# Stick-breaking attention: one set of products with values per pair of heads, q and k split once and copied by DMA, scan in place

## The chip, the cores and the metric

The program runs on one core of a Trainium2 chip: TensorE (PE) multiplies matrices, VectorE (DVE) and ScalarE (ACT) work elementwise, GpSimd (POOL) and SyncE (SP) issue most transfers. The metric is device time in microseconds, the median of three executions.

## The reference

Four sub-layers run on 512 tokens of width 1024: retention, a gated ConvFFN, stick-breaking attention, a second ConvFFN. The change touches the third alone. It has 16 heads of 64 columns; for each block of 128 queries the blocks of keys are swept from the last to the first:

```python
z = jnp.einsum('bhqd,bhkd->bhqk', qb, kb) * scale
log1m = jnp.where(mask, jax.nn.log_sigmoid(-z), 0.0)
excl = lax.cumsum(log1m, axis=3, reverse=True) - log1m
log_a = jax.nn.log_sigmoid(z) + excl + suffix[..., None]
a = jnp.where(mask, jnp.exp(log_a), 0.0)
acc = acc + jnp.einsum('bhqk,bhkd->bhqd', a, vb)
```

Each weight is thus sigmoid(z) of its key times the product of sigmoid(-z) over the keys between it and the query. Everything is float32.

## The kernel before

Activations lie transposed, features on partitions, tokens along the row. A float32 product that is to be exact is made of three products on rounded parts: hi = the operand cast to fp32r, lo = the rest (`split`, `parts`, `mm3`). Weights arrive in 512 KB pieces by SyncE (`chunk`) and are split by ScalarE (L130) and VectorE (L131).

The heads are worked in eight pairs, here called pair 0 to pair 7. A step is one head of a pair with one block of 128 queries, so a pair has eight steps, from the longest row of keys (four blocks, 512) to the shortest (one block, 128). In a step, `sb_weights` makes z with two products (L591), two sigmoids (L593, L594), a scan on VectorE that multiplies sigmoid(-z) up from the right end (L597, into tile cs) and the product of both (L601). One step later `sb_transpose` turns the blocks on TensorE (L609) and copies them out (L610, over the tile of sigmoid(-z)). `sb_av` multiplies them with the values (L617) once both heads of a query block are there: `o` gathers 128 columns of queries at a time, the first head on partitions 0 to 63, the second on 64 to 127. After the last block `o` is split into hi and lo (L108, L109).

q and k of a pair (`sb_qk`) are 128 rows, 64 for each head. A product for z has 128 partitions: q's hi above its lo, against k's hi twice and then k's lo twice. So for every head hi is cast (L558, and L562 for the second copy of k) and lo is subtracted (L560, L563) on 64 partitions at a time: six casts and six subtractions per pair.

Between the steps, `sb_fill` gives TensorE other work: in pairs 0 to 5 q and k for the pair two ahead, in pairs 0, 2 and 4 values as well, in pairs 6 and 7 the output projection. `FILL` is how many pieces go into each step. The program's instructions are recorded and then ordered by a scheduler, so the order on each engine is not that of the code; each engine works its own list strictly in order. Buffers come from pools that hand out a fixed number per tag: a tile waits until the last reader of its buffer is done. GpSimd's queue issues, early in the program, copies and sums of FFN weights (tile sum); in the attention it only sets one column of cs to zero per step (L596).

Of the kernel before, what the change touches and what calls it, by code (L numbers as in the profile page):

```python
# [9 lines left out]
F32 = mybir.dt.float32  # L10
# [5 lines left out]
P = 128  # L16
# [20 lines left out]
class Kernel:  # L37
# [12 lines left out]
    def __init__(self, ctx, tc, t):  # L50
        self.tc, self.nc, self.t = tc, tc.nc, t
        self.const = ctx.enter_context(tc.tile_pool(name="const", bufs=1))
        self.wp = ctx.enter_context(tc.tile_pool(name="wp", bufs=1))
        self.ap = ctx.enter_context(tc.tile_pool(name="ap", bufs=1))
        self.dp = ctx.enter_context(tc.tile_pool(name="dp", bufs=1, space=bass.MemoryType.DRAM))
        self.ps = ctx.enter_context(tc.tile_pool(name="ps", bufs=1, space=bass.MemoryType.PSUM))
        self.n = 0
        self.pp = None
        self.att_pool()
        self.phase("mix")  # L60

    def att_pool(self):
        self.pa = self.tc.tile_pool(name=self.name("pa"), bufs=1, space=bass.MemoryType.PSUM, reuse_waits="tile")
# [17 lines left out]
        return f"{s}_{self.n}"  # L81

    BUFS = {"xh": 8, "xl": 8, "tt": 8, "rr": 2}
    PHASE = {"qk": 8, "vv": 8, "yy": 16, "pp": 8, "cs": 4, "ar": 2, "oh": 5, "ol": 5}

    def sb(self, tag, cols=S, dt=F32):
        pool, bufs = (self.ap, self.BUFS) if tag in self.BUFS else (self.ph, self.PHASE)
# [432 lines left out]
    def ffn(self, l, last):  # L520
# [11 lines left out]
                s += 1  # L532
        self.swap_pool()
        self.down(l, a, s, last)
        self.phase("mix" if last is not None else None)
        return a


    def sb_qk(self, p, out, first=None):
# [3 lines left out]
        for i in range(2):  # L543
# [8 lines left out]
                    yield  # L552
            x = self.sb("tt")
            nc.vector.tensor_mul(x, ps, self.r)
            for e in range(2):
                own, other = slice(e * DH, e * DH + DH), slice(DH - e * DH, 2 * DH - e * DH)
                hi = self.sb("qk", S, F32R)
                nc.scalar.copy(hi[own], x[own])  # L558
                lo = hi if i == 0 else self.sb("tt", S, F32R)
                nc.vector.tensor_sub(lo[other], x[own], hi[own].bitcast(F32))  # L560
                if i == 1:
                    nc.scalar.copy(hi[other], x[own])  # L562
                    nc.vector.tensor_sub(lo[own], x[own], hi[own].bitcast(F32))  # L563
                heads[e] += [hi] if i == 0 else [hi, lo]
        out.append(heads)

    def sb_v(self, c, out):
# [15 lines left out]
    def sb_weights(self, qk, i, e):  # L583

        nc = self.nc
        n = (i + 1) * P
        nz = max(n, 256)
        q, kh, kl = qk[e]
        z = self.psum("z", 2)
        for m, k in enumerate((kh, kl)):  # L590
            nc.tensor.matmul(z[:, :nz], q[:, i * P : (i + 1) * P], k[:, :nz], start=m == 0, stop=m == 1)  # L591
        sg, bt = self.sb("pp"), self.sb("pp")
        nc.scalar.activation(sg[:, :n], z[:, :n], AF.Sigmoid, scale=-0.125)  # L593
        nc.scalar.activation(bt[:, :n], z[:, :n], AF.Sigmoid, scale=0.125)  # L594
        left = self.sb("cs", S + P)
        nc.gpsimd.memset(left[:, n : n + 1], 0.0)  # L596
        nc.vector.tensor_tensor_scan(  # L597
            left[:, :n][:, ::-1], sg[:, :n][:, ::-1], self.diag[:, S - n :][:, ::-1],
            0.0, op0=ALU.mult, op1=ALU.max,
        )  # L600
        nc.vector.tensor_mul(bt[:, :n], bt[:, :n], left[:, 1 : n + 1])  # L601
        return sg, bt

    def sb_transpose(self, i, sg, bt):
        nc = self.nc
        n = (i + 1) * P
        tp = self.psum("tp", 2)
        for j in range(i + 1):
            nc.tensor.transpose(tp[:, j * P : (j + 1) * P], bt[:, j * P : (j + 1) * P], self.ident)  # L609
        nc.vector.tensor_copy(sg[:, :n], tp[:, :n])  # L610
        return sg

    def sb_av(self, o, p, i, v, aT):
        for j in range(i + 1):
            for e in range(2):
                h = (2 * p + e) % 8
                self.nc.tensor.matmul(  # L617
                    o[e * DH : (e + 1) * DH, i * P : (i + 1) * P], v[p // 4 * NT + j][:, h * DH : (h + 1) * DH],
                    aT[e][:, j * P : (j + 1) * P], start=j == 0, stop=j == i,
                )  # L620

    def stick_breaking(self):


        first = self.first4("sfirst")
        qk, v, os = [], [], []
        self.rc = self.token_major_r()
        for p in range(2):
            for _ in self.sb_qk(p, qk, first[2 * p : 2 * p + 2]):
                pass  # L630
# [1 line left out]
            pass  # L632
        self.swap_pool()
        steps = [(p, i, e) for p in range(NPAIR) for i in reversed(range(NT)) for e in range(2)]
        wt, aT, fill, o = {}, {}, iter(()), None
        for t in range(len(steps) + 2):
            if t < len(steps):
                p, i, e = steps[t]
# [4 lines left out]
                wt[t] = self.sb_weights(qk[p], i, e)  # L643
            for _ in range(rate):
                next(fill, None)
            if 1 <= t <= len(steps):
                aT[t - 1] = self.sb_transpose(steps[t - 1][1], *wt.pop(t - 1))
            if t >= 2 and steps[t - 2][2] == 1:
                p, i, _ = steps[t - 2]
                if i == NT - 1:  # L650
                    o = self.one()
                self.sb_av(o, p, i, v, (aT.pop(t - 3), aT.pop(t - 2)))
                if i == 0:
                    os.append(self.split(o, ("yy", "yy")))
        for _ in fill:
            pass
        self.swap_pool()
# [189 lines left out]
```

## Time and profile before

| | |
|---|---|
| runs | 1377.50, 1377.51, 1378.72 us; median 1377.51 |
| profiled execution | 1378.58 us, span 1376.8 us |
| PE, share of the span busy | 99% (7208 matmuls) |
| DVE | 74%, 1014.2 us |
| ACT | 45%, 618.8 us |
| POOL | 4%, 51.4 us |
| TensorE clock granted | 0.999 of 2.4 GHz |

The shares are means over stages with different limits. A matmul's busy time includes its way through the array, so the next one starts well before it ends; what TensorE really needs is read from the starts. Times of instructions are from one profiled execution, 1.1 us above the median.

### The profile page before, as it was taken

What the parts mean: (1) busy time and instruction counts of PE and PEld (TensorE: products, weight loads), DVE (VectorE), ACT (ScalarE), POOL (GpSimd) and SP (SyncE); (2) the same over time, 40 slices, a digit from 0 to 9 for tenths busy, and PEclk for the clock granted to TensorE, in tenths of its full rate; (3) what the DMA queues carried; (4) which work ended last, traced back from release to release, by engine and by line L of the source; (5) the groups of instructions that cost most, each with busy time, mean ns of one, the idle gap of its engine ahead of it and who ended that gap; (6) DMA issues with size and microseconds to landing.
All of it is one profiled execution on the core that took longest, in us unless ns stands there. A gap on an engine that the chain in (4) does not pass through costs nothing.

```text
span 1376.8 us, 18478 instructions
## 1 busy us (share of the span) xinstructions
PE 1364.9 (99%) x7208; PEld 1157.4 (84%) x7208; DVE 1014.2 (74%) x1416; ACT 618.8 (45%) x876; POOL 51.4 (4%) x134
## 2 busy tenths in 40 slices
PE   9999999999999999999999999999999999999997
PEld 7888888888888889889988888787788899889887
DVE  7774564664769877678667779889789886787765
ACT  6443333433346444344344655554356443444434
POOL 1222210000000000000000000000000000000000
PEclk9999999999999999999999999999999999999999
DMA  8999983131233335324522421120133335235121
GB/s 301 312 281 273 276 220 96 49 115 62 64 94 119 107 108 179 112 92 124 164 72 69 138 92 51 58 62 24 39 123 122 101 117 181 74 105 182 54 69 62
DMA packets 53190, 170.22 MB, mean 124 GB/s; under 512 B 6000, under 2 KB 8176, under 8 KB 53104
## 3 DMA queue, kind: packets, MB, share of 16 engines
q1 hardware_dynamic: 42880, 136.25, 30.9%
q0 software_dynamic: 8704, 31.46, 9.3%
q10 hardware_dynamic: 1520, 1.33, 0.3%
q8 instruction: 57, 0.93, 0.3%
q14 instruction: 29, 0.24, 0.1%
HBM read 166.92 MB, written 33.55 MB: 146 GB/s over the span
## 4 chain that ended last, share of the span: by engine, by line
PE 96%; DVE 3%; issue 0%; ACT 0%; DVEq 0%
PE acc L139 23%; PE acc L137 23%; PE acc L138 23%; PE x L455 6%; PE att L137 4%; PE att L138 4%; PE att L139 4%; PE z L455 3%; PE acc L455 2%; PE one L617 2%; PE z L591 1%; PE tp L609 1%; DVE cs L597 1%; DVE lo L131 0%; DVE tt L563 0%; DVE tt L560 0%
## 5 line engine op out<-in xcount | busy, mean ns | idle before, releaser
L130 ACT CAST hi<-raw 128x1024 fp32r<-128x1024 f32 (+2 forms) x277 | 268.3, 969 | 432.4 <-PE acc L138 274.5
L138 PE MATMUL acc<-xl,hi 128*128 128x512 f32 x960 | 374.5, 390 | 0.0
L139 PE MATMUL acc<-xh,lo 128*128 128x512 f32 x960 | 374.4, 390 | 0.0
L137 PE MATMUL acc<-xh,hi 128*128 128x512 f32 x960 | 374.2, 390 | 0.0
L131 DVE TENSOR_TENSOR lo<-raw,hi 128x1024 fp32r<-128x1024 f32 (+2 forms) x277 | 309.4, 1118 | 55.4 <-ACT hi L130 53.7
L139 PEld LDWEIGHTS acc<-xh,lo 128*128 128x128 f32 x960 | 180.2, 188 | 37.5 <-issue 0.5
L137 PEld LDWEIGHTS acc<-xh,hi 128*128 128x128 f32 x960 | 180.3, 188 | 36.8 <-issue 0.5
L138 PEld LDWEIGHTS acc<-xl,hi 128*128 128x128 f32 x960 | 180.3, 188 | 36.0
L407 DVE SCALAR_TENSOR_TENSOR tt<-tt,vec,tt 128x511 f32<-128x511 f32 (+1 forms) x176 | 131.3, 747 | 4.0 <-ACT tt L405 1.4
L404 DVE TENSOR_TENSOR tt<-acc,rr 128x512 f32<-128x512 f32 x80 | 55.1, 688 | 75.6 <-PE acc L139 75.6
L189 DVE TENSOR_TENSOR x<-x,acc 128x512 f32<-128x512 f32 x72 | 48.9, 685 | 53.5 <-PE acc L139 53.5
L139 PE MATMUL acc<-hi,xl 128*128 128x512 f32 (+1 forms) x256 | 86.0, 336 | 0.0
L138 PE MATMUL acc<-lo,xh 128*128 128x512 f32 (+1 forms) x256 | 85.9, 336 | 0.0
L137 PE MATMUL acc<-hi,xh 128*128 128x512 f32 (+1 forms) x256 | 85.9, 336 | 0.0
L405 ACT ACTIVATE tt<-tt,vec 128x512 f32<-128x512 f32 x88 | 71.5, 812 | 11.0 <-DVE tt L404 10.0
L139 PE MATMUL acc<-yy,lo 128*128 128x512 f32 x192 | 75.2, 392 | 0.0
L137 PE MATMUL acc<-yy,hi 128*128 128x512 f32 x192 | 75.1, 391 | 0.0
L138 PE MATMUL acc<-yy,hi 128*128 128x512 f32 x192 | 75.0, 391 | 0.0
L455 PE MATMUL x<-oh,hi 128*128 128x256 f32 x240 | 68.2, 284 | 0.0
L455 PE MATMUL x<-ol,hi 128*128 128x256 f32 x240 | 67.9, 283 | 0.0
L455 PE MATMUL x<-oh,lo 128*128 128x256 f32 x240 | 67.9, 283 | 0.0
L597 DVE TENSOR_TENSOR_SCAN cs<-pp,diag 128x512 f32<-128x512 f32 (+3 forms) x64 | 52.1, 819 | 3.3 <-ACT pp L593 2.2
(173 smaller groups left out, 2254.7 us busy)
## 6 DMA issues: line engine op xcount, KB each, us to landing
raw<-in_up SPq DMA_DIRECT2D x80, 512.0 KB, 3.9
sum<-in_fast POOLq DMA_DIRECT2D x36, 512.0 KB, 8.7
raw<-sum SPq DMA_DIRECT2D x24, 512.0 KB, 3.4
raw<-in_fast SPq DMA_DIRECT2D x18, 512.0 KB, 3.6
raw<-in_rv SPq DMA_DIRECT2D x16, 512.0 KB, 6.0
raw<-in_rg SPq DMA_DIRECT2D x16, 512.0 KB, 4.3
raw<-in_rout SPq DMA_DIRECT2D x16, 512.0 KB, 4.2
raw<-in_rqk SPq DMA_DIRECT2D x12, 512.0 KB, 6.3
```

Source lines behind the costliest of these rows:

```text
L130: nc.scalar.copy(hi, raw)
L131: nc.vector.tensor_sub(lo, raw, hi.bitcast(F32))
L137: mm(out, a[0], b[0], start=start, stop=False)
L138: mm(out, a[0], b[1], start=False, stop=False)
L139: mm(out, a[1], b[0], start=False, stop=stop)
L189: self.nc.vector.tensor_add(self.x[m], self.x[m], ps)
L404: nc.vector.tensor_mul(u, ps, self.r)
L405: nc.scalar.activation(c, u, AF.Identity, scale=w[2], bias=w[3])
L407: nc.vector.scalar_tensor_tensor(c[:, i:], u[:, : S - i], w[2 - i], c[:, i:], op0=ALU.mult, op1=ALU.add)
L455: mm(out[:, :Q], a[ai], b[bi], start=start and k + i == 0, stop=k == nk - 1 and i == 2, skip_group_check=not start)
L597: nc.vector.tensor_tensor_scan(left[:, :n][:, ::-1], sg[:, :n][:, ::-1], self.diag[:, S - n :][:, ::-1], 0.0, op0=ALU.mult, op1=ALU.max,)
L617: self.nc.tensor.matmul(o[e * DH : (e + 1) * DH, i * P : (i + 1) * P], v[p // 4 * NT + j][:, h * DH : (h + 1) * DH], aT[e][:, j * P : (j + ...
```

## The change

The cast of q or k to hi and the subtraction for lo are made once for both heads, on 128 partitions, into one tile hl (hi in the first 512 columns, lo behind it; one buffer). GpSimd's queue then copies the 64 rows of a head to where z wants them: for q four copies of 64 x 512 (hi to the upper, lo to the lower half, for each head), for k four of 64 x 1024 (hi and lo together, to both halves, for each head).

The scan writes over its own input, a tile sg that is kept for each of the eight steps and has one column of zeros behind it, set once. bt has two buffers.

The transposed weights of a head go into one tile `at` for all four query blocks, laid out so that what stands against one block of keys is contiguous: 512 queries for the first block, 384, 256 and 128 for the others. `sb_av` runs once per pair, behind the second step of the next pair, with eight products. The tiles of this phase have a pool of their own, and the results of the later four pairs take buffers xh and xl.

```diff
@@ -81,7 +81,7 @@
         return f"{s}_{self.n}"
 
     BUFS = {"xh": 8, "xl": 8, "tt": 8, "rr": 2}
-    PHASE = {"qk": 8, "vv": 8, "yy": 16, "pp": 8, "cs": 4, "ar": 2, "oh": 5, "ol": 5}
+    PHASE = {"qk": 8, "vv": 8, "yy": 16, "pp": 8, "cs": 4, "ar": 2, "oh": 5, "ol": 5, "sq": 2, "sk": 4, "hl": 1, "bt": 2, "at": 2, "oo": 8}
 
     def sb(self, tag, cols=S, dt=F32):
         pool, bufs = (self.ap, self.BUFS) if tag in self.BUFS else (self.ph, self.PHASE)
@@ -532,7 +532,7 @@
                 s += 1
         self.swap_pool()
         self.down(l, a, s, last)
-        self.phase("mix" if last is not None else None)
+        self.phase("sb" if last is not None else None)
         return a
 
 
@@ -552,16 +552,23 @@
                     yield
             x = self.sb("tt")
             nc.vector.tensor_mul(x, ps, self.r)
-            for e in range(2):
-                own, other = slice(e * DH, e * DH + DH), slice(DH - e * DH, 2 * DH - e * DH)
-                hi = self.sb("qk", S, F32R)
-                nc.scalar.copy(hi[own], x[own])
-                lo = hi if i == 0 else self.sb("tt", S, F32R)
-                nc.vector.tensor_sub(lo[other], x[own], hi[own].bitcast(F32))
-                if i == 1:
-                    nc.scalar.copy(hi[other], x[own])
-                    nc.vector.tensor_sub(lo[own], x[own], hi[own].bitcast(F32))
-                heads[e] += [hi] if i == 0 else [hi, lo]
+            hl = self.sb("hl", 2 * S, F32R)
+            nc.scalar.copy(hl[:, :S], x)
+            nc.vector.tensor_sub(hl[:, S:], x, hl[:, :S].bitcast(F32))
+            move = lambda to, of: nc.gpsimd.dma_start(to, of)
+            if i == 0:
+                q = self.sb("sq", 2 * S, F32R)
+                for e in range(2):
+                    own = slice(e * DH, e * DH + DH)
+                    for a in range(2):
+                        move(q[a * DH : a * DH + DH, e * S : e * S + S], hl[own, a * S : a * S + S])
+                    heads[e].append(q[:, e * S : e * S + S])
+            else:
+                for e in range(2):
+                    k = self.sb("sk", 2 * S, F32R)
+                    for a in range(2):
+                        move(k[a * DH : a * DH + DH], hl[e * DH : e * DH + DH])
+                    heads[e] += [k[:, :S], k[:, S:]]
         out.append(heads)
 
     def sb_v(self, c, out):
@@ -589,42 +596,49 @@
         z = self.psum("z", 2)
         for m, k in enumerate((kh, kl)):
             nc.tensor.matmul(z[:, :nz], q[:, i * P : (i + 1) * P], k[:, :nz], start=m == 0, stop=m == 1)
-        sg, bt = self.sb("pp"), self.sb("pp")
+        sg, bt = self.sg[i][e], self.sb("bt")
         nc.scalar.activation(sg[:, :n], z[:, :n], AF.Sigmoid, scale=-0.125)
         nc.scalar.activation(bt[:, :n], z[:, :n], AF.Sigmoid, scale=0.125)
-        left = self.sb("cs", S + P)
-        nc.gpsimd.memset(left[:, n : n + 1], 0.0)
+
         nc.vector.tensor_tensor_scan(
-            left[:, :n][:, ::-1], sg[:, :n][:, ::-1], self.diag[:, S - n :][:, ::-1],
+            sg[:, :n][:, ::-1], sg[:, :n][:, ::-1], self.diag[:, S - n :][:, ::-1],
             0.0, op0=ALU.mult, op1=ALU.max,
         )
-        nc.vector.tensor_mul(bt[:, :n], bt[:, :n], left[:, 1 : n + 1])
-        return sg, bt
-
-    def sb_transpose(self, i, sg, bt):
+        nc.vector.tensor_mul(bt[:, :n], bt[:, :n], sg[:, 1 : n + 1])
+        return bt
+
+
+    ROW = S - P
+
+    def sb_transpose(self, i, bt, aT):
         nc = self.nc
         n = (i + 1) * P
         tp = self.psum("tp", 2)
         for j in range(i + 1):
             nc.tensor.transpose(tp[:, j * P : (j + 1) * P], bt[:, j * P : (j + 1) * P], self.ident)
-        nc.vector.tensor_copy(sg[:, :n], tp[:, :n])
-        return sg
-
-    def sb_av(self, o, p, i, v, aT):
-        for j in range(i + 1):
+        to = aT[:, i * P : i * P + (i + 1) * self.ROW].rearrange("p (j q) -> p j q", q=self.ROW)[:, :, :P]
+        nc.vector.tensor_copy(to, tp[:, :n].rearrange("p (j q) -> p j q", q=P))
+
+    def sb_av(self, o, p, v, aT):
+        for j in range(NT):
             for e in range(2):
                 h = (2 * p + e) % 8
                 self.nc.tensor.matmul(
-                    o[e * DH : (e + 1) * DH, i * P : (i + 1) * P], v[p // 4 * NT + j][:, h * DH : (h + 1) * DH],
-                    aT[e][:, j * P : (j + 1) * P], start=j == 0, stop=j == i,
+                    o[e * DH : (e + 1) * DH, j * P :], v[p // 4 * NT + j][:, h * DH : (h + 1) * DH],
+                    aT[e][:, j * (P + self.ROW) : j * self.ROW + S], start=j == 0, stop=j == NT - 1, skip_group_check=True,
                 )
 
     def stick_breaking(self):
 
 
+        nc = self.nc
         first = self.first4("sfirst")
         qk, v, os = [], [], []
         self.rc = self.token_major_r()
+        self.sg = [[self.ph.tile([P, (i + 1) * P + 1], F32, name=f"sg{i}{e}") for e in range(2)] for i in range(NT)]
+        for i in range(NT):
+            for e in range(2):
+                nc.gpsimd.memset(self.sg[i][e][:, (i + 1) * P :], 0.0)
         for p in range(2):
             for _ in self.sb_qk(p, qk, first[2 * p : 2 * p + 2]):
                 pass
@@ -632,7 +646,7 @@
             pass
         self.swap_pool()
         steps = [(p, i, e) for p in range(NPAIR) for i in reversed(range(NT)) for e in range(2)]
-        wt, aT, fill, o = {}, {}, iter(()), None
+        wt, fill = {}, iter(())
         for t in range(len(steps) + 2):
             if t < len(steps):
                 p, i, e = steps[t]
@@ -643,15 +657,14 @@
                 wt[t] = self.sb_weights(qk[p], i, e)
             for _ in range(rate):
                 next(fill, None)
+            if t % 8 == 1 and t > 8:
+                o = self.one()
+                self.sb_av(o, t // 8 - 1, v, aT)
+                os.append(self.split(o, ("oo", "oo") if len(os) < 4 else ("xh", "xl")))
             if 1 <= t <= len(steps):
-                aT[t - 1] = self.sb_transpose(steps[t - 1][1], *wt.pop(t - 1))
-            if t >= 2 and steps[t - 2][2] == 1:
-                p, i, _ = steps[t - 2]
-                if i == NT - 1:
-                    o = self.one()
-                self.sb_av(o, p, i, v, (aT.pop(t - 3), aT.pop(t - 2)))
-                if i == 0:
-                    os.append(self.split(o, ("yy", "yy")))
+                if t % 8 == 1:
+                    aT = [self.sb("at", (NT + 1) * self.ROW) for _ in range(2)]
+                self.sb_transpose(steps[t - 1][1], wt.pop(t - 1), aT[steps[t - 1][2]])
         for _ in fill:
             pass
         self.swap_pool()
```

On TensorE, the end of pair 0's longest query blocks before: a transpose (tp), the first eight products with values (one), and the next z.

```order
L609 MATMUL tp_6722<-diag,pp_6646 128x128 x3
L617 MATMUL one_6727<-pp_6554,vv_6439 64x128
L617 MATMUL one_6727<-pp_6602,vv_6439 64x128
L617 MATMUL one_6727<-pp_6554,vv_6466 64x128
L617 MATMUL one_6727<-pp_6602,vv_6466 64x128
L617 MATMUL one_6727<-pp_6554,vv_6493 64x128
L617 MATMUL one_6727<-pp_6602,vv_6493 64x128
L617 MATMUL one_6727<-pp_6554,vv_6520 64x128
L617 MATMUL one_6727<-pp_6602,vv_6520 64x128
L591 MATMUL z_6736<-qk_6393,qk_6385 128x256
L591 MATMUL z_6736<-tt_6395,qk_6385 128x256
```

The same engine in the change, at the only products of pair 0; z and tp are those of pair 1.

```order
L139 MATMUL acc_6877<-xh_6074,lo_6874 128x512
L626 MATMUL one_6901<-at_6644,vv_6453 64x512
L626 MATMUL one_6901<-at_6645,vv_6453 64x512
L626 MATMUL one_6901<-at_6644,vv_6480 64x384
L626 MATMUL one_6901<-at_6645,vv_6480 64x384
L626 MATMUL one_6901<-at_6644,vv_6507 64x256
L626 MATMUL one_6901<-at_6645,vv_6507 64x256
L626 MATMUL one_6901<-at_6644,vv_6534 64x128
L626 MATMUL one_6901<-at_6645,vv_6534 64x128
L618 MATMUL tp_6916<-diag,bt_6866 128x128 x4
L598 MATMUL z_6922<-sk_6435,sq_6425 128x384 x2
```

Eight products of 128 columns stood here for one block of queries, and three more such groups for the others; now eight products of 512 to 128 columns stand behind the second z of the next pair and ahead of its first transpose.

On VectorE, the end of pair 0 before: k for pair 2 is scaled (L554), its four subtractions follow (L560, L563) between the last copies of pair 0 and the first scan of pair 1 (the order names a scan SCALAR_TENSOR_TENSOR).

```order
L554 TENSOR_TENSOR tt_6877<-acc_6830,rr_6308 128x512
L610 COPY pp_6808<-tp_6870 128x128
L131 TENSOR_TENSOR lo_7337<-raw_7334,hi_7336 128x1024
L560 TENSOR_TENSOR tt_6881<-tt_6877,qk_6879 64x512
L563 TENSOR_TENSOR tt_6881<-tt_6877,qk_6879 64x512
L560 TENSOR_TENSOR tt_6887<-tt_6877,qk_6885 64x512
L563 TENSOR_TENSOR tt_6887<-tt_6877,qk_6885 64x512
L597 SCALAR_TENSOR_TENSOR cs_6898<-pp_6894,diag 128x512
```

In the change, the same stretch, from the scaling of k for pair 2 to the second scan of pair 1.

```order
L554 TENSOR_TENSOR tt_6852<-acc_6812,rr_6308 128x512
L620 COPY at_6644<-tp_6849 128x128
L131 TENSOR_TENSOR lo_7259<-raw_7256,hi_7258 128x1024
L603 SCALAR_TENSOR_TENSOR sg_6389<-sg_6389,diag 128x512
L620 COPY at_6645<-tp_6884 128x128
L607 TENSOR_TENSOR bt_6866<-bt_6866,sg_6389 128x512
L557 TENSOR_TENSOR hl_6854<-tt_6852,hl_6854 128x512
L603 SCALAR_TENSOR_TENSOR sg_6390<-sg_6390,diag 128x512
```

The four subtractions are one (L557), and it stands behind the first scan and its product.

On ScalarE, ahead of the first pair before: casts of weights (hi), then the six casts for pair 0's q and k, then the first block of values (vv).

```order
L130 CAST hi_6570<-raw_6568 128x1024
L558 CAST qk_6385<-tt_6383 64x512
L558 CAST qk_6388<-tt_6383 64x512
L558 CAST qk_6393<-tt_6391 64x512
L562 CAST qk_6393<-tt_6391 64x512
L558 CAST qk_6399<-tt_6391 64x512
L562 CAST qk_6399<-tt_6391 64x512
L130 CAST hi_6750<-raw_6748 128x1024
L581 ACTIVATE vv_6439<-acc_6440,rc_6381 128x256
```

In the change: hl of q, a weight, the first block of values, hl of k.

```order
L130 CAST hi_6581<-raw_6579 128x1024
L556 CAST hl_6401<-tt_6399 128x512
L130 CAST hi_6742<-raw_6740 128x1024
L588 ACTIVATE vv_6453<-acc_6454,rc_6381 128x256
L556 CAST hl_6411<-tt_6409 128x512
L588 ACTIVATE vv_6480<-acc_6481,rc_6381 128x256
```

The cast of k's hl, which waits for the copies of q's hl, stands between the first and the second block of values.

## Rows read from the trace of the kernel before

**Rows 1.** Stretches by pair of heads; the first row names the columns.
```profile
core 0: us, PE busy (x) PEld busy (x) DVE busy (x) ACT busy (x) POOL busy (x), PEclk, DMA share, GB/s
789.41:819.44 30.03, 30.03 (x218) 26.62 (x216) 22.51 (x32) 15.56 (x30) 0.79 (x8) 1.00 0.28 88
819.44:840.74 21.30, 21.17 (x126) 15.35 (x124) 20.50 (x36) 12.17 (x26) 0.79 (x8) 1.00 0.16 50
840.74:871.58 30.84, 30.84 (x223) 27.09 (x221) 24.78 (x38) 15.97 (x32) 0.79 (x8) 1.00 0.24 69
...
944.99:966.56 21.57, 20.88 (x126) 15.44 (x124) 20.51 (x36) 10.56 (x24) 0.79 (x8) 1.00 0.08 25
966.56:987.79 21.23, 20.76 (x133) 15.91 (x131) 19.00 (x35) 8.59 (x20) 0.39 (x4) 1.00 0.09 26
```

**Rows 2.** TensorE in order of time: start, us, engine, line, tile.
```profile
820.02 0.40 PE L137 MATMUL acc<-xh,hi 128*128 128x512 f32 x1
820.25 0.40 PE L138 MATMUL acc<-xl,hi 128*128 128x512 f32 x1
...
823.47 0.43 PE L617 MATMUL one<-pp,vv 128*64 128x128 f32 x2
823.83 0.44 PE L591 MATMUL z<-qk,qk 128*128 128x384 f32 x1
```

**Rows 3.** The same, two places ahead of those.
```profile
803.79 1.09 PE L617 MATMUL one<-pp,vv 128*64 128x128 f32 x16
804.81 0.39 PE L591 MATMUL z<-qk,qk 128*128 128x256 f32 x1
...
818.85 0.66 PE L617 MATMUL one<-pp,vv 128*64 128x128 f32 x8
819.44 0.50 PE L591 MATMUL z<-qk,qk 128*128 128x512 f32 x1
```

**Rows 4.** Chain that ended last, from 819 us on: start, us, what.
```profile
819.74 1.23 DVE lo L131
821.00 0.69 DVE tt L560
...
823.81 1.23 DVE cs L597
825.27 0.43 PE one L617 x2
```

**Rows 5.** DVE by line, 789.41 to 987.79 us: busy us, mean ns, idle before.
```profile
L597 DVE TENSOR_TENSOR_SCAN cs<-pp,diag 128x512 f32<-128x512 f32 (+3 forms) x64 | 52.1, 819 | 3.3 <-ACT pp L593 2.2
L601 DVE TENSOR_TENSOR pp<-pp,cs 128x512 f32<-128x512 f32 (+3 forms) x64 | 31.2, 488 | 4.0
L610 DVE COPY pp<-tp 128x512 f32<-128x512 f32 (+3 forms) x64 | 30.8, 481 | 5.8 <-PE tp L609 5.5
L131 DVE TENSOR_TENSOR lo<-raw,hi 128x1024 fp32r<-128x1024 f32 (+1 forms) x24 | 28.1, 1173 | 1.4 <-ACT hi L130 1.1
```

**Rows 6.** ScalarE, VectorE before the first pair, in order of time.
```profile
776.50 1.28 DVE L554 TENSOR_TENSOR tt<-att,rr 128x512 f32<-128x512 f32 x2
...
777.21 1.91 ACT L558 CAST qk<-tt 64x512 fp32r<-64x512 f32 x3 [1.00 <-DVE tt L554]
...
782.01 0.46 ACT L581 ACTIVATE vv<-acc,rc 128x256 f32<-128x256 f32 x1
...
789.41 0.40 PE L591 MATMUL z<-qk,qk 128*128 128x512 f32 x1
```

**Rows 7.** GpSimd's DMA issues, 150 to 195 us: ns min/median/max.
```profile
L518 POOL DMA_DIRECT2D sum<-sum x6: 515/546/838, 151.0 to 188.3; - x6
```

**Rows 8.** DMAs of the whole span: KB each, median us to landing.
```profile
raw<-in_sfirst SPq DMA_DIRECT2D x8, 256.0 KB, 2.5
...
sum<-sum POOLq DMA_DIRECT2D x4, 384.0 KB, 5.5
```

**Rows 9.** Engines in that stretch, columns as in rows 1.
```profile
150.00:195.00 45.00, 45.00 (x216) 37.86 (x216) 28.76 (x40) 18.99 (x26) 12.66 (x18) 1.00 0.97 253
```

More of the change, by code (lines that the diff above doesn't have):

```diff
@@ L59, in __init__ @@
         self.att_pool()
-        self.phase("mix")
+        self.phase("ret")
     def att_pool(self):
```

## The prediction

> **What bounds the kernel now.** I read the stretches by pair of heads first, then the chain of waits, then TensorE (PE) and VectorE (DVE) instruction by instruction. Everything that the change touches lies between the first product of pair 0, at 789.41 us, and the last products with values, at about 988 us; the rest of the program keeps its instructions. The reader should see two kinds of pair [rows 1]. Pairs 0, 2 and 4, which also project values, take 30.0 to 30.8 us, and DVE is busy in 22.5 to 24.8 of them: TensorE sets their length. Pairs 1, 3 and 5 (one of three that are alike is shown) and pairs 6 and 7 take 21.2 to 21.6, and DVE is busy in 20.5 of 21.3 in the odd ones. There DVE is full or nearly so. That TensorE looks 99% busy everywhere says little, since matmuls overlap: one starts 0.23 us after another and is shown with 0.40 [rows 2].
>
> The chain of waits says the same. At the start of each odd pair it leaves TensorE and runs through DVE alone for 6 us: a weight split, then four subtractions of the k tile (lines 560 and 563, 0.69 us each; the two in the middle are left out), then a scan, and only then a product with values [rows 4]. These four subtractions are what the change takes off that chain.
>
> What DVE has to do in a pair follows from its totals over eight pairs [rows 5]: scans 52.1/8 = 6.5, products with the scan 31.2/8 = 3.9, copies of transposes 30.8/8 = 3.85; together 14.3. To that comes, in an odd pair, two weight splits of 1.2, two scalings, six subtractions and one split of the result at 0.69 each: 2.4 + 6.2 = 8.6, in all 22.9. Only 20.5 fit into the 21.3 us, so some 2.4 us slip into the next pair, which has room.
>
> **Products with values.** A product on f32 appears as two records, so a pair has 40 records of 128 columns. A run of 16 takes 804.81 - 803.79 = 1.02 us, one of 8 takes 0.59 [rows 3], one of 2 takes 0.36 [rows 2]. The slope is 0.054 per record and 0.16 is left per run; that two records alone take 0.36 fits 0.107 for a record that nothing overlaps, and half of that in a run, where the two heads write different halves of the partitions. Before, the 160 products stand in 43 runs on TensorE; in the change there are 8 runs, one per pair. The columns stay: 40 x 0.054 = 2.16. By count of records it would be 16 x 0.054 + 0.16 = 1.0 us per pair, which I exclude because 512 columns cost 0.23 even in one pass [rows 2]. I take 2.16 + 0.16, and 0.32 more, since the first record now streams four times as many columns with no partner (0.43 instead of 0.107): 2.64 us. In an even pair the four runs (2, 8, 6 and 4 products) cost 0.38 + 1.02 + 0.81 + 0.59 = 2.80, so the gain is 0.2, not the 12 saved instructions' worth.
>
> The run also moves: the products of pair p now stand behind the second z of pair p + 1. Pair 0 loses 1.02 + 0.81 + 0.59 = 2.4 us, and is bound by TensorE, so it gets shorter by that; behind pair 7 the whole 2.64 stands in place of one run of 0.38, which is 2.3 us more with nothing to overlap. These nearly cancel.
>
> **Hi and lo of q and k.** Per pair the six subtractions of 64 partitions become two of 128, and six casts on ScalarE become two. DVE time goes by columns, so each keeps 0.69: DVE loses 4 x 0.69 = 2.75 us per pair. An odd pair then holds 22.9 - 2.75 = 20.2 us of DVE work. TensorE's need there is 48 x 0.23 = 11.0 for the fill, 2.5 for z (5,632 columns at the same rate), 20 transposes at 0.107 = 2.1 and 2.64: 18.3 us. Lower end 18.3, upper end 21.3 as now; I take 20.0, nearer to DVE's row, since only two buffers of bt are left and z of a step can no longer run ahead of the transposes two steps back, where before there was room for four. That is 1.3 us in each of pairs 1, 3 and 5. Pair 6 now begins with five DVE instructions left over from pair 7's q and k; without four of those it gains 1.4. Pair 7 has no such work; I give it 0.5 for the backlog that it no longer inherits (between 0 and 2.0).
>
> The casts saved on ScalarE (6 x 0.64 to 2 x 0.64 [rows 6]) are worth nothing by themselves: ScalarE is busy in half of each pair [rows 1]. The 64 memsets that go are 0.8 us of GpSimd per pair [rows 1], which has nothing else to do there. The scan in place keeps its columns and its mean of 0.82 [rows 5].
>
> **The added copies.** GpSimd issues four DMAs behind each subtraction, 64 in all. One issue takes 0.55 [rows 7]. How long one takes to land is not in this trace. Below stands 2.5 us, a load of 256 KB by SyncE's queue; above stands 5.5, a 384 KB copy by this same queue [rows 8], measured while the DMA engines were 0.97 busy [rows 9]. In these pairs they are 0.08 to 0.28 busy [rows 1], so I take 3.3, near the lower end. The Trainium skill's page "DMA: Bandwidth & Descriptors" (Anatomy of one DMA) fits 2.0 us plus bytes over 436 GB/s to this path, an estimate of 2.6 us for 256 KB; by it the stall below is nil and the sum 0.5 us better; no run here shows it yet.
>
> There is one hl buffer, so the cast of the next tile waits in ScalarE's queue until all four copies of the last have landed, and sigmoids and values stand behind it. Between pairs' uses a whole pair (21 us or more) passes, so only the start is tight. There, q's subtraction follows three scalings from 776.50 at 0.64 each [rows 6] and ends at 779.2; with a landing time L its fourth copy lands at 779.2 + 1.65 + L; then k's cast (0.64), its subtraction (0.69) and a second copy (issued 0.55 later, L to land) give about 782.7 + 2L. TensorE asks for it at 789.41, when the value projection of block 0 is through [rows 6]. So it is on time up to L = 3.35, and then costs 2L - 6.7. I put 0.5 us.
>
> **The sum.** Pair 0 -2.4; pairs 1, 3, 5 -3.9; pairs 2 and 4 -0.4; pair 6 -1.4; pair 7 -0.5; behind the pairs +2.3; start +0.5: -5.8 us. The profiled execution took 1378.6 us (span 1376.8); 1372.8 would be its successor. It lies 1.1 above the median of 1377.5, so I predict 1371.7.
>
> **Rivals.**
> A: DVE was all that held the odd pairs, and they fall to TensorE's 18.3 to 18.7, pairs 6 and 7 too: -2.4 - 7.8 - 0.4 - 2.9 - 2.0 + 2.3 = -13.2, about 1364.3. For it: 20.5 of 21.3 us busy. Against: DVE's 20.2 us must then slip by nearly 2 us again, with fewer buffers.
> B: the wait for DVE is replaced by the tighter chain z, sigmoid, scan, transpose through two buffers; the odd pairs stay at 21.3. Then -2.4 - 0.4 + 2.3 + 0.5 = 0, or up to -3 with pair 6: 1374.5 to 1377.5.
> C, the other side: the copies land late. For L = 6 the start stalls 5.3 us. In pairs 0, 2 and 4 the cast of k follows that of q by 24 matmuls (5.5) and some 1.5 us of z and transposes, while q needs 0.69 + 0.64 + 0.69 + 1.65 + L; ScalarE, and with it the next sigmoid, waits L - 4.0 = 2.0 there, three times. 5.3 + 6.0 - 6.3 = +5, about 1382.5. It decides from L = 5 on; against it stands the idle DMA, for it the 5.5 us row. DVE could also hold up GpSimd's issue: an issue reaches 838 ns against a least of 515 [rows 7] with DVE busy in 28.8 of 45 us [rows 9], 0.3 us at worst, 1.3 per group of four, which alone does not reach L = 5. The Trainium skill's page "SBUF — State Buffer" (The "DVE blocks DMA" trap) says that such DMAs get no descriptors while DVE runs certain fast copies, 620 ns becoming 3100; that would be this rival outright. The trace speaks against it here, as 515 to 838 ns shows.
>
> **How the numbers follow.** Forecast (-3 to -10 us) 0.53, A 0.15, B 0.18, C 0.14. What a measurement can tell from no change is about 0.2%, 2.75 us. Faster than 1374.8: A and nearly all of the forecast, 0.65; slower than 1380.3: C with L above 5.5, 0.12; the rest, B above all, 0.23. The range runs from A's 1364.3 to 1380.5, leaving out most of C and the far end of A; the forecast's own is 1367.5 to 1374.5.
>
> **What would show it.** Right: 16 subtractions of line 557 at 0.69, 8 runs of products near 2.6 us, odd pairs near 20, the copies landing in 2.5 to 4 us, the first z at 789 to 790. Wrong: odd pairs still at 21.3 with TensorE waiting at the transposes (B); a gap ahead of the first z, or ScalarE idle before the casts of line 556 until a DMA (C); pairs 2 and 4 much shorter than 30.4, which would mean that a run costs more than the 0.16 I read.

## Result and profile after: 0.9% faster, twice the gain of the forecast

The changed kernel takes 1366.28 us (median of four runs, 1365.08 to 1366.55) against 1377.75 for the kernel before on the same chip: ratio 0.9914, 95% interval 0.9897 to 0.9931, or 11.5 us. The forecast was 1371.7. The profiled execution took 1366.12 us, its span 1363.8 where it was 1376.8; readings of single pairs below come from one such execution each.

The stretches by pair of heads answer to [rows 1] (same columns): pairs 0, 1, 2, 6 and 7.

```profile
789.33:816.38 27.05, 27.05 (x182) 24.68 (x180) 21.40 (x31) 15.04 (x30) 6.13 (x12) 1.00 0.64 167
816.38:835.77 19.39, 18.67 (x102) 14.07 (x101) 18.28 (x31) 9.74 (x22) 2.54 (x6) 1.00 0.51 130
835.77:865.48 29.71, 29.71 (x199) 25.96 (x197) 21.58 (x33) 13.31 (x28) 5.55 (x12) 1.00 0.50 128
...
933.83:952.49 18.66, 18.50 (x103) 14.14 (x101) 17.94 (x31) 8.95 (x21) 3.00 (x6) 1.00 0.48 114
952.49:975.17 22.68, 22.18 (x123) 15.90 (x121) 19.95 (x37) 9.37 (x20) 0.00 (x0) 1.00 0.10 27
```

Every pair is shorter but the last, and pair 0 begins at 789.33 where it began at 789.41, so the start costs nothing that shows. The DMA share of pairs 0 to 6 rises from 0.08 to 0.28 [rows 1] to between 0.45 and 0.64. In us, from each pair's first z to the next one's, with two experiments (below) that do one half of the change each:

| | start | 0 | 1 | 2 | 3 | 4 | 5 | 6 | 7 to end of products | sum |
|---|---|---|---|---|---|---|---|---|---|---|
| forecast | +0.5 | -2.4 | -1.3 | -0.2 | -1.3 | -0.2 | -1.3 | -1.4 | +1.8 | -5.8 |
| the change | -0.1 | -3.0 | -1.9 | -1.1 | -1.9 | -1.1 | -2.0 | -2.9 | +1.4 | -12.6 |
| products per pair alone | -0.5 | -3.0 | -0.5 | -1.1 | -0.5 | -1.1 | +0.3 | -1.4 | +1.4 | -6.5 |
| hl and copies alone | +1.3 | +0.1 | -1.4 | 0.0 | -1.4 | 0.0 | -0.8 | -1.1 | -0.1 | -3.4 |

TensorE in order of time at the only products of pair 0, which answers to [rows 2, 3]:

```profile
820.03 0.39 PE L139 MATMUL acc<-xh,lo 128*128 128x512 f32 x1
820.35 2.37 PE L626 MATMUL one<-at,vv 128*64 128x512 f32 x16
822.65 0.66 PE L618 MATMUL tp<-diag,bt 128*128 128x128 f32 x4
```

The run lasts 822.65 - 820.35 = 2.30 us. Weight products start 0.23 apart [rows 2]; the run starts 0.32 behind the last of them, 0.09 more.

VectorE by line over the eight pairs, which answers to [rows 5]:

```profile
L603 DVE TENSOR_TENSOR_SCAN sg<-sg,diag 128x512 f32<-128x512 f32 (+3 forms) x64 | 52.3, 818 | 2.0 <-ACT sg L600 1.2
L620 DVE COPY at<-tp 128x512 f32<-128x512 f32 (+3 forms) x64 | 30.8, 482 | 8.6 <-PE tp L618 8.4
L557 DVE TENSOR_TENSOR hl<-tt,hl 128x512 fp32r<-128x512 f32 x14 | 9.6, 685 | 1.0 <-ACT hl L556 0.9
```

Scan and copies keep their times; the copy into the strided tile costs 482 ns where it was 481. The 128-partition subtraction takes 685 ns, as reckoned.

The chain of waits in pair 1 (start, us, what), beside [rows 4]:

```profile
820.41 2.30 PE one L626 x16
...
823.34 0.69 DVE at L620
...
833.30 0.42 DVE bt L607
833.86 0.41 PE tp L618 x2
```

It still enters VectorE and stays there for 10 us, but no subtractions stand at its head any more. VectorE is busy in 18.28 of 19.39 us. TensorE waits for it only 0.7 us in this pair, in two places late in it (ahead of the transposes at 831.55 and 833.86), so its own list is nearly as long; neither engine alone sets the pair.

ScalarE at the start, beside [rows 6]:

```profile
782.56 0.62 ACT L556 CAST hl<-tt 128x512 fp32r<-128x512 f32 x1 [1.20 <-DMA sq<-hl]
```

k's cast waited 1.20 us for q's copies and was still early enough: the first z stands at 789.33. GpSimd's issues (ns min/median/max), who waited for the copies (us, times), and the landing times (KB each, median us), beside [rows 7, 8]:

```profile
L558 POOL DMA_DIRECT2D sq<-hl x32: 509/517/556, 778.1 to 934.3; - x32
...
  ACT hl L556: 4.3, 5
```

```profile
sk<-hl POOLq DMA_DIRECT2D x32, 256.0 KB, 4.4
...
sq<-hl POOLq DMA_DIRECT2D x32, 128.0 KB, 2.8
```

No issue takes over 556 ns, with VectorE busy in 18.28 of 19.39 us in an odd pair, so nothing shows that VectorE holds the issues up. The Trainium skill's page "SBUF — State Buffer" (The "DVE blocks DMA" trap) describes such a hold-up during certain fast copies of VectorE; the issues here show none. The 256 KB copies land in 4.4 us and the 128 KB ones in 2.8, between the two bounds that were set from [rows 8]. The Trainium skill's page "DMA: Bandwidth & Descriptors" (Anatomy of one DMA) would put them at an estimated 2.6 and 2.3 us; the measured times, with four issued in a row and loads beside them, are longer.

### The profile page after: what moved, and what is told of

Same layout as the page of the kernel before. It is cut to its first block, busy times and chain, and to the rows that moved or that the text cites. A ratio compares the mean times of both kernels' runs of the same rounds, so it can differ in the third digit from the quotient of the medians.

```text
span 1363.8 us, 18143 instructions
## 1 busy us (share of the span) xinstructions
PE 1350.7 (99%) x7016; PEld 1147.6 (84%) x7016; DVE 991.1 (73%) x1384; ACT 599.0 (44%) x844; POOL 78.3 (6%) x142
## 4 chain that ended last, share of the span: by engine, by line
PE 95%; DVE 4%; issue 0%; ACT 0%; DVEq 0%; ACTq 0%
PE acc L138 23%; PE acc L137 23%; PE acc L139 23%; PE x L455 6%; PE att L137 4%; PE att L138 4%; PE att L139 4%; PE z L455 3%; PE acc L455 2%; PE one L626 1%; PE z L598 1%; DVE sg L603 1%; PE tp L618 1%; DVE at L620 1%; DVE bt L607 1%
## 5 line engine op out<-in xcount | busy, mean ns | idle before, releaser
L138 PE MATMUL acc<-xl,hi 128*128 128x512 f32 x992 | 386.8, 390 | 0.0
L137 PE MATMUL acc<-xh,hi 128*128 128x512 f32 x992 | 386.5, 390 | 0.0
L139 PE MATMUL acc<-xh,lo 128*128 128x512 f32 x992 | 386.5, 390 | 0.0
L139 PEld LDWEIGHTS acc<-xh,lo 128*128 128x128 f32 x992 | 186.2, 188 | 38.5
L137 PEld LDWEIGHTS acc<-xh,hi 128*128 128x128 f32 x992 | 186.3, 188 | 38.1 <-DVE x L189 0.4
L138 PEld LDWEIGHTS acc<-xl,hi 128*128 128x128 f32 x992 | 186.3, 188 | 37.5 <-issue 0.2
L603 DVE TENSOR_TENSOR_SCAN sg<-sg,diag 128x512 f32<-128x512 f32 (+3 forms) x64 | 52.3, 818 | 2.0 <-ACT sg L600 1.2
L137 PEld LDWEIGHTS acc<-hi,xh 128*128 128x128 f32 x256 | 48.4, 189 | 5.3
L138 PEld LDWEIGHTS acc<-lo,xh 128*128 128x128 f32 x256 | 48.4, 189 | 5.3
L139 PEld LDWEIGHTS acc<-hi,xl 128*128 128x128 f32 x256 | 48.5, 189 | 4.9
```

What stands on the lines that cost most here:

```text
L137: mm(out, a[0], b[0], start=start, stop=False)
L138: mm(out, a[0], b[1], start=False, stop=False)
L139: mm(out, a[1], b[0], start=False, stop=stop)
L603: nc.vector.tensor_tensor_scan(sg[:, :n][:, ::-1], sg[:, :n][:, ::-1], self.diag[:, S - n :][:, ::-1], 0.0, op0=ALU.mult, op1=ALU.max,)
```

## Experiments

**The halves of the change.** First the products per pair with the old casts and subtractions.

```diff
-            nc.scalar.copy(hl[:, :S], x)
-            nc.vector.tensor_sub(hl[:, S:], x, hl[:, :S].bitcast(F32))
...
+            for e in range(2):
...
+                nc.scalar.copy(hi[own], x[own])
...
+                nc.vector.tensor_sub(lo[other], x[own], hi[own].bitcast(F32))
...
```

> The change with the old casts and subtractions of q and k (no copies by DMA); products once per pair and the scan in place stay. Theory (both parts gain, about half each): even pairs stay near 29.8 us, odd pairs rise from 19.4 to 20.5-21 because VectorE has 22.9 us of work in them again; about 1371 us. Rival R (only the fewer runs of products count): 1366-1367. Rival D (only VectorE's relief counts): 1375-1377.

1371.66 us (1371.26 to 1372.2), ratio 0.9954 (0.9942 to 0.9967). Then the copies, with the products per block of queries as before.

```diff
...
-            if t % 8 == 1 and t > 8:
...
-                self.sb_av(o, t // 8 - 1, v, aT)
...
+            if t >= 2 and steps[t - 2][2] == 1:
...
+                self.sb_av(o, p, i, v, (aT.pop(t - 3), aT.pop(t - 2)))
...
```

> The change with the products with values per block of queries, as before (46 runs on TensorE instead of 8); the copies by DMA and the scan in place stay. Theory (both parts gain): even pairs back to 30.7, odd pairs near 20.2; 1371-1373 us. Rival R (only the runs count): 1376-1378. Rival D (only VectorE's relief): 1366-1368.

1374.51 us (1373.23 to 1375.73), ratio 0.9974 (0.9965 to 0.9984): 1.5 us over what was expected, with a start 1.3 late and less from pairs 5 and 6. The trace has 32 runs, not 46. The rows of the table say which pair each half shortens: the products take 3.0 and 1.1 from the pairs that TensorE sets, where the copies do nothing; in pairs 1 and 3 the two add up (0.5 + 1.4 = 1.9). In pairs 5 and 6 they give 2.0 us more together than singly, and the start differs by 1.8 between these two kernels; what joins them there was not taken apart.

The 1.4 us of the copies in an odd pair are not VectorE's alone, since TensorE's list changes with them. Its products with values in pair 1, in the kernel before (behind the first run, which is in [rows 2]) and then with the copies alone:

```profile
825.27 0.43 PE L617 MATMUL one<-pp,vv 128*64 128x128 f32 x2
...
829.29 0.43 PE L617 MATMUL one<-pp,vv 128*64 128x128 f32 x2
...
830.56 0.66 PE L617 MATMUL one<-pp,vv 128*64 128x128 f32 x8
...
831.62 0.65 PE L617 MATMUL one<-pp,vv 128*64 128x128 f32 x6
...
835.52 0.88 PE L617 MATMUL one<-pp,vv 128*64 128x128 f32 x12
...
840.15 0.66 PE L617 MATMUL one<-pp,vv 128*64 128x128 f32 x8
```

```profile
825.25 0.44 PE L627 MATMUL one<-at,vv 128*64 128x128 f32 x4
...
830.45 1.09 PE L627 MATMUL one<-at,vv 128*64 128x128 f32 x16
...
835.47 0.88 PE L627 MATMUL one<-at,vv 128*64 128x128 f32 x12
...
840.07 0.66 PE L627 MATMUL one<-at,vv 128*64 128x128 f32 x8
```

Seven runs became four. By the lengths in [rows 2, 3] and 0.19 a run outside them (shown below, where a run is cut in two) that is 3.55 + 7 x 0.19 = 4.88 us against 2.80 + 4 x 0.19 = 3.56, an estimate of 1.3 of the 1.4 us. No run takes the subtractions off VectorE and keeps TensorE's order, so how much of the 1.4 is VectorE's shorter list itself stays open. What is shown is that fewer runs alone do not give it: with the products per pair and the old subtractions an odd pair has two runs, yet gains only 0.5, with VectorE busy in 20.43 of 20.79 us (columns as in rows 1):

```profile
815.92:836.71 20.79, 20.01 (x102) 14.54 (x101) 20.43 (x34) 12.74 (x26) 0.00 (x0) 1.00 0.16 51
```

Third, the scan in place alone, in the kernel before.

```diff
...
-            left[:, :n][:, ::-1], sg[:, :n][:, ::-1], self.diag[:, S - n :][:, ::-1],
+            sg[:, :n][:, ::-1], sg[:, :n][:, ::-1], self.diag[:, S - n :][:, ::-1],
...
```

> The kernel before with nothing but the scan in place (a tile per step, zeros set once, no memset per step). Theory: the scan keeps its 0.82 us and nobody waited for the memsets: 1377.7 us, within 1.5. Rival (the buffers' waits cost something): 1373 or less.

1377.65 us, ratio 0.9998 (0.9989 to 1.0007): nothing, as expected.

**What a run of products costs.** The eight products of a pair in two runs, three weight products between them.

```diff
...
+                self.sb_av(o, t // 8 - 1, v, aT, (0, 1))
+            next(fill, None)
+            if t % 8 == 1 and t > 8:
+                self.sb_av(o, t // 8 - 1, v, aT, (2, 3))
```

> The change with each pair's run of eight products with values cut in two runs of four (28 and 12 records), three weight products (0.69 us of TensorE) between them; the same instructions otherwise. Theory (pairs 2 and 4 fell by 1.1 us because they have three runs fewer, so that a run costs (1.13)/3 = 0.38 us beyond its columns): pairs 2 and 4 rise from 29.71 to 30.0 to 30.1 us, pair 0 from 27.05 alike, odd pairs by 0.2 to 0.4; 1368 to 1369.5 us. Rival (a run costs the 0.16 us that was read from two runs of the kernel before, and the 1.1 us come from something else): pairs 2 and 4 at 29.85 to 29.9; 1366.5 to 1367.7 us.

1369.49 us (1369.1 to 1370.88), ratio 0.994 (0.9926 to 0.9954). Pairs 2 and 4 rise from 29.71 and 29.73 to 30.06: a run costs 0.33 to 0.35. TensorE in pair 2 of that kernel, where weight products of 256 columns start 0.12 apart, shows where it sits:

```profile
842.42 0.28 PE L139 MATMUL acc<-hi,xl 128*128 128x256 f32 x1
842.63 1.72 PE L626 MATMUL one<-at,vv 128*64 128x512 f32 x8
844.29 0.39 PE L137 MATMUL acc<-hi,xh 128*128 128x256 f32 x1
844.51 0.28 PE L138 MATMUL acc<-lo,xh 128*128 128x256 f32 x1
...
845.19 0.87 PE L626 MATMUL one<-at,vv 128*64 128x256 f32 x8
845.99 0.66 PE L618 MATMUL tp<-diag,bt 128*128 128x128 f32 x4
```

The first run of 28 records lasts 1.66 us and the second, of 12, 0.80: 0.054 a record and 0.15 over. But it begins 0.21 behind the weight product ahead of it, 0.09 late, and the first weight product behind it holds the next one up for 0.22, 0.10 late. 0.15 + 0.09 + 0.10 = 0.34. The odd pairs rose by 0.7, more than the 0.4 expected. TensorE's waits for VectorE stay at 0.7 us in pair 1, so a delay of TensorE's there is not taken up by them; that it also delays the copies that VectorE makes of the next transposes fits this but was not tried.

Then the same products by head, all of the first and then all of the second, so that neighbours no longer write different partitions.

```diff
-        for j in range(NT):
-            for e in range(2):
+        for e in range(2):
+            for j in range(NT):
```

> The change with the products with values in the order of heads (all four key blocks of the first head of a pair, then all four of the second) instead of alternating, so that two neighbouring records no longer use different halves of the output's columns. Theory (the products are short because two 64-column records of different column halves run beside each other): a run of products rises from 2.30 us to about 4.3 us (40 records at 0.107), +2.0 us on TensorE in each of the 8 pairs; in the odd pairs half of that is covered since VectorE sets their length, so 1379 to 1382 us. Rival (the order of heads does not matter, only the number of runs of products): 2.3 us a run as before, 1365 to 1367 us.

1378.45 us (1377.29 to 1379.44), ratio 1.0004 (0.9995 to 1.0013). A run takes 3.86 us:

```profile
821.22 3.93 PE L626 MATMUL one<-at,vv 128*64 128x512 f32 x16
825.08 0.66 PE L618 MATMUL tp<-diag,bt 128*128 128x128 f32 x4
```

So alternating the heads is worth 1.56 us a run, over the eight pairs as much as the whole change; 3.86 is less than the 4.3 expected, (3.86 - 0.15)/40 = 0.093 for a record instead of 0.107. By head, neighbours also add into the same columns of the output; but the transposes of the change, which don't, take 0.10 a record too (four in 823.06 - 822.65 = 0.41 us), so this is not needed to explain the slower rate. Odd pairs rose by 1.55 like the even ones, although VectorE's work there stayed at 18.28 us: no half of it was covered.

**What holds the odd pairs.** First bt in eight buffers.

```diff
...
-        sg, bt = self.sg[i][e], self.sb("bt")
+        sg, bt = self.sg[i][e], self.sb("tt")
```

> The change with the transposed weights (bt) in the buffers of the tag tt, of which there are eight, instead of in two buffers of their own. Theory (odd pairs are set by VectorE's own work, not by the two buffers): odd pairs stay at 19.2 to 19.4 us, 1365 to 1367 us. Rival (the chain of rival B, transposes that wait for a buffer of bt to be read by the products, holds each pair): pairs shorten by 0.3 to 0.8 us each, 1360 to 1364 us.

1366.25 us (1366.02 to 1366.82), ratio 0.9915: no change, with pairs 1, 3 and 5 at 19.69, 19.42 and 19.02. The two buffers of bt, part of rival B, hold nothing. Next, half of the copies of transposes on ScalarE.

```diff
...
-                self.sb_transpose(steps[t - 1][1], wt.pop(t - 1), aT[steps[t - 1][2]])
+                self.sb_transpose(steps[t - 1][1], wt.pop(t - 1), aT[steps[t - 1][2]], (nc.vector.tensor_copy, nc.scalar.copy)[steps[t - 1][2]])
```

> The change with the copies of transposed weights of every second head on ScalarE instead of VectorE (32 copies of about 0.69 us each leave VectorE: 4 in each pair). Theory (after the change VectorE sets the odd pairs, 18.3 busy of 19.4 us, with TensorE's need at 18.3 close behind): odd pairs fall to 18.4 to 18.8 us, even pairs unchanged (TensorE's), 1362 to 1364 us. Rival (the chain from split to scan to copy is a chain of latency, and ScalarE's queue puts the copy later): odd pairs longer, 1367 to 1370 us.

1364.5 us (1363.45 to 1365.31), ratio 0.9899 (0.9884 to 0.9914). Pair 1 falls to 18.83 us (columns as in rows 1):

```profile
817.39:836.22 18.83, 18.47 (x103) 14.09 (x101) 16.88 (x27) 11.17 (x26) 2.53 (x6) 1.00 0.50 135
```

VectorE is now busy in 16.88 of it and TensorE waits for it 0.4 us, once, so 18.8 is nearly all TensorE's own list. Pair 3 falls alike, to 18.84, but pair 5 does not (19.34 where it was 19.24).

The other way round, VectorE gets work back: four subtractions of 64 partitions per pair that nobody reads. First reading hl, in all pairs:

```diff
+            for e in (0, 1, 0)[: 1 + 2 * i]:
+                own = slice(e * DH, e * DH + DH)
+                nc.vector.tensor_sub(self.sb("tt")[own], x[own], hl[own, :S].bitcast(F32))
```

> The change with four subtractions of 64 partitions per pair of q and k added on VectorE that nobody reads (one behind q, three behind k), so that VectorE has the work of before and ScalarE, GpSimd and TensorE that of the change. Theory (odd pairs are held by VectorE): odd pairs 20.4, pair 6 about 20, even pairs unchanged: 1370-1371 us. Rival R (only the runs on TensorE count): 1366-1367.

1376.17 us (1374.46 to 1376.93), ratio 0.9984 (0.9975 to 0.9993): a miss, and a useful one. The odd pairs rise by 1.1 to 2.4 and pair 6 by 0.8, but pair 0 begins at 795.37, 6.0 us late, and takes 25.85 us where it took 27.05. The engines around it (columns as in rows 1):

```profile
786.00:795.37 9.37, 9.37 (x81) 9.37 (x80) 5.52 (x7) 4.17 (x7) 2.04 (x4) 1.00 0.65 151
795.37:799.00 3.63, 0.76 (x5) 0.33 (x4) 1.89 (x3) 2.70 (x4) 1.40 (x3) 1.00 0.81 281
799.00:802.62 3.62, 3.62 (x17) 3.48 (x18) 3.12 (x4) 1.98 (x5) 0.63 (x2) 0.53 0.55 109
...
795.37:821.22 25.85, 22.98 (x132) 19.97 (x130) 21.92 (x35) 13.58 (x27) 6.13 (x12) 0.93 0.57 156
```

TensorE is busy all the way to the late first z, so the 6.0 us are no stall. Its list is in another order: 50 products for values (0.12 us each, 6.0 in all) that stand in pair 0 in the change (182 records there, 132 here) stand ahead of z. What was lost comes behind z: TensorE stands idle for 2.9 us, and then works 3.6 us at a mean granted clock of 0.53, near the lower of its levels of 1.2 and 2.4 GHz, which costs an estimated 3.62 x (1 - 0.53) = 1.7 us. Start and pair 0 together are 4.8 us longer. The chain to that wait (start, us, what), and the z that waited:

```profile
779.73 7.45 DMA sq<-hl
...
787.28 0.63 ACT hl L556
...
790.54 5.63 DMA sk<-hl
```

```profile
798.86 0.98 PE L601 MATMUL z<-sk,sq 128*128 128x512 f32 x2 [2.87 <-DVE tt L554]
```

k's cast waits for the last of q's copies, k's own copies are issued only from 788.98 on, the cast for pair 1 waits for the last of these, and the next z waits for VectorE's work behind that cast (L554). This is rival C's chain, through the one buffer of hl. A first z in its old place would have had to wait as well: k's second copy was issued at 789.5, and copies there take 3.4 to 5.6 us. q's copies (landing, us min/median/max) in this kernel and in the change, and SyncE's loads of values (issue start, us) in both:

```profile
DMA to landing us min/median/max: 6.1/7.5/7.5
```

```profile
DMA to landing us min/median/max: 2.5/2.7/2.7
```

```profile
778.30 3.26 SPq L122 DMA_DIRECT2D raw<-in_sv  x2
```

```profile
780.68 1.43 SPq L122 DMA_DIRECT2D raw<-in_sv  x2
```

GpSimd issued the four copies from 778.15 on in this kernel and from 778.11 on in the change. What is seen to differ beside them is SyncE's queue: the first of two loads of 512 KB starts at 778.30 here and at 780.68 there, the second at 781.23 and 781.78. The loads land late here too, after 7.6 and 7.0 us, where they took 3.8 and 4.7. That the earlier load is the cause was not tried by itself.

The same subtractions without reading hl, for the pairs from 2 on:

```diff
+            for e in () if first else (0, 1, 0)[: 1 + 2 * i]:
+                nc.vector.tensor_sub(self.sb("tt")[own], x[own], self.r[own])
```

> The change with four unread 64-partition subtractions (of the f32 value and its rounded value, without reading hl) put back on VectorE in the pairs 2 to 7 alone, so that the start is untouched. Theory (the odd pairs and pair 6 are set by VectorE's work, so what the removed subtractions took comes back there): pairs 3 and 5 rise from 19.3 to 20.2 to 20.6 us, pair 6 from 18.7 to 20.0, the even pairs and the start unchanged; 1369 to 1371.5 us. Rival (the removed work on VectorE is no part of the gain): all pairs unchanged, 1365 to 1367 us.

1378.27 us (1376.94 to 1381.68), ratio 1.0005: 12 us where 3 to 5 were expected. In the profiled execution, which took 1380.7 us, pairs 1 and 3 take 23.4 and 23.3 us, and pairs 2, 4 and 6, too, are 1.9, 0.9 and 3.0 longer. The chain in pair 1, and the engines in two stretches of it:

```profile
814.84 5.19 DMA sq<-hl
...
820.13 0.63 ACT hl L556
...
822.22 0.41 PE tp L621 x2
```

```profile
818.34:822.22 3.88, 2.06 (x7) 0.78 (x6) 2.65 (x6) 1.60 (x3) 0.44 (x1) 1.00 0.13 24
822.22:826.00 3.78, 3.78 (x17) 2.04 (x17) 2.90 (x4) 0.00 (x0) 1.61 (x4) 0.69 0.83 189
```

The last of q's copies takes 5.19 us, k's cast waits for it in ScalarE's queue, its subtraction waits for the cast in VectorE's, and the product with the scan stands behind that, so TensorE idles 1.8 us. Behind the idle time the granted clock is 0.69 for 3.8 us, a mean between the two levels of 1.2 and 2.4 GHz. So spread them, one at a time:

```diff
+                    if k % 4 == 1:
+                        own = slice(k // 4 * DH, k // 4 * DH + DH)
+                        nc.vector.tensor_sub(self.sb("tt")[own], self.r[own], self.r[own])
```

> The change with the same four unread 64-partition subtractions per prepared pair (pairs 2 to 7) on VectorE, now one at a time, spread between the key and query products instead of two or three in a row ahead of a scan, and on values that are long there. Theory (VectorE's sum of work sets the odd pairs): 4 x 0.6 = 2.4 us more on VectorE in each of them, less the 1.1 us that it stood idle: pairs 1, 3 and 5 rise from 19.3 to 20.6 to 21.5 us, pair 6 from 18.7 to 19.5 to 20.5, the even pairs and the start unchanged, no stretch at a lower granted clock; 1370 to 1374 us. Rival (in the run before it was only the row of three ahead of a scan, with the wait of 1.8 us and the lower clock behind it, that cost time): all pairs unchanged, 1365 to 1367 us.

1374.07 us (1373.31 to 1375.16), ratio 0.9972 (0.9961 to 0.9982). Pair 1 of it, and what TensorE waits for in all pairs (us, times, longest):

```profile
815.85:837.41 21.56, 19.59 (x103) 13.84 (x101) 20.12 (x34) 10.18 (x22) 2.96 (x7) 1.00 0.45 114
```

```profile
PE tp L621 <- DVE bt L610: 7.2, 14, 1.0
```

VectorE is busy 1.84 us longer than in the change and the pair is 2.17 longer, at full clock and with one run of products as in the change. TensorE's waits for bt rise from 2.7 to 7.2 us. So work on VectorE does lengthen pairs 1 and 3 (21.55); pair 5 rose only to 19.97, less than expected. Pair 2 rose by 1.4, which was not expected: with this on top, TensorE's pairs are no longer free of VectorE.

**A faster version.** The copies on ScalarE together with two buffers of hl.

```diff
...
-"hl": 1, "bt": 2, "at": 2
+"hl": 2, "at": 2
...
```

> The change with every second head's copies on ScalarE, as before this run, and with two buffers of hl (transposed weights in the eight buffers of tt, to make room). Theory (what is left in the odd pairs is TensorE's own need; hl's single buffer lets the cast wait 4.3 us in five places, all of them hidden): 1363.5 to 1365.5 us, odd pairs 18.8, start 789 to 790. Rival (the single hl buffer holds the start and pairs 5 and 6): start 786 to 788, pair 5 18.8, 1359 to 1362 us.

1363.63 us (1362.99 to 1364.16), ratio 0.9895 (0.9881 to 0.9908): its runs lie below all runs of the change (the kernel before took 1378.18 beside it and 1377.75 beside the change). They overlap with those of the copies on ScalarE alone (1363.45 to 1365.31), so what the second buffer of hl adds is not shown. TensorE's waits for bt fall to 1.1 us in three places (2.7 in eight in the change). Of the 2.7 us of profile between them, 0.7 is an earlier pair 0, and that start lies anywhere from 788.3 to 790.2 in kernels that don't touch it.

## Why the prediction was right, and where its sizes were off

Direction and places held; the sum was half of what came. The measured 1366.28 lies inside the stated range but below the forecast's own stretch of 1367.5 to 1374.5; the range reached that far down because of rival A, whose price for the odd pairs did not come. That much is luck.

- The term that was mis-sized is the price of a run of products. It was read from the length of the runs [rows 2, 3] as 0.16 + 0.054 a record. The inside is right (0.15 measured), but 0.09 ahead and 0.10 behind are booked to the neighbours; cutting one run in two shows 0.33 to 0.35 in all. The 0.32 added for a first record without a partner isn't there: the new run is 2.30 = 40 x 0.054 + 0.14, not 2.64. With both, an even pair saves (2.80 + 4 x 0.19) - (2.30 + 0.19) = 1.07, measured 1.1, forecast 0.2; pair 0 saves 2.4 + 3 x 0.19 = 3.0, measured 3.0. The prediction named this as what would show it wrong: pairs 2 and 4 shorter than 30.4.
- The odd pairs' 1.3 came out in size: the copies alone give 1.4, to 19.9 where 20.0 was taken. Its reason is only half shown. The prediction gave it to VectorE's shorter list and took the products at nothing there, with TensorE's need at 18.3. But before, TensorE's list was as full: weight products, z and transposes as in the prediction's sum, 15.6, and the seven runs, 4.88, make an estimated 20.5 of 21.3 us, as much as VectorE's 20.5. The copies alone bring both down, to an estimated 19.2 and a measured 18.4; the change brings them to an estimated 18.1 and a measured 18.3. So the match is partly luck. And the pair is not just the longer of two sums: with VectorE's work unchanged, 1.56 us more of products on TensorE lengthened the odd pairs by 1.55. Pair 6 gains 1.1 from the copies, 1.4 from the products, 2.9 together.
- Start and landing times: forecast 0.5 us late, measured 0.1 early, where the start scatters from 788.3 to 790.2 in kernels that don't touch it. The cast into hl waited for copies in five places, 4.3 us in all, not at the start alone; none of it shows in TensorE's waits. 3.3 us for a landing lay between the 2.8 and 4.4 found. Behind the pairs: +1.8 forecast, +1.4 measured.
- Rival A in its pure form is not it: pairs 1, 3 and 5 are at 19.2 to 19.4, not 18.3 to 18.7, and pairs 1 and 3 reach 18.8 only with VectorE relieved again. For pair 6 its 2.9 was right (18.66 us). Its total of 1364.3 lies nearer than the forecast's because the even pairs, to which it gave 0.4 in all, gave 2.2, and pair 0 0.6 more than its 2.4. Rival B is out: odd pairs are at 19.4, not 21.3, and eight buffers for bt change nothing. Rival C's chain is real and was near: it stalls TensorE in two kernels, by 2.9 us behind landing times of 7.45 and 5.63, and by 1.8 behind one of 5.19.

## What to carry to other kernels

Price a short run of an unlike kind of matmul by the starts of its neighbours, not by its own length: here 0.19 of 0.34 us was outside. Where two engines are both nearly full, count both lists, and look whether relief of one also changes the order on the other. Before a late start is called a stall, look what the engine did in the meantime. A copy by DMA that replaces work of an engine can land much later in a kernel that differs little: look what the load queue sends in the same microseconds, and what stands in the queues behind whoever waits for the copy.

## What had not been expected of the hardware

Four copies issued at the same time land in 2.5 to 2.7 us in one kernel and in 6.1 to 7.5 in another, where the first of two loads beside them was issued 2.4 us earlier; what else may differ was not tried. Records that use one half of the output partitions take 3.86 us a run and alternating ones 2.30. Two idle stretches on TensorE, of 2.9 and 1.8 us, were followed by 3.6 and 3.8 us at mean granted clocks of 0.53 and 0.69.
